# Issuing the first two loads of an add-and-GELU kernel ahead of the program's opening barrier

## The chip, the cores and the metric

The kernel runs on one core of a Trainium2 chip. The metric is the device time of one execution in microseconds (us); lower is better. The profile's span runs from the first to the last instruction that it shows. The device time is longer than the span (123.23 against 121.5 us before the change).

## The reference

```python
def reference(x, y):                       # both (1024, 4096) float32
    z = x + y
    return 0.5 * z * (1 + np.tanh(np.sqrt(2 / np.pi) * (z + 0.044715 * z ** 3)))
```

Two inputs of 16.8 MB are read and one output of 16.8 MB is written.

## The kernel before

Each of the 128 partitions holds 32768 numbers. The data are loaded in five pieces per input and stored in five pieces, all issued by SyncE on one queue (a transfer is issued when SyncE orders it, and lands when its last data have arrived). The compute goes through 32 chunks of 128x1024: an add on GpSimd (only the first chunk is on VectorE), a square on ScalarE, `scalar_tensor_tensor` on VectorE, a sigmoid on ScalarE, a multiply on VectorE. `z` has room for the whole problem; `y` has two buffers, so only the loads of the last two pieces of y (and their followers in the queue) wait for compute.

```python
    loads = [2048, 6144, 8192, 8192, 8192]      # columns per piece: 1, 3, 4, 4, 4 MB
    stores = [8192, 8192, 8192, 4096, 4096]
    ...
    pool_y = ctx.enter_context(tc.tile_pool(name="y", bufs=2))
    ...
    def load_x(i):
        a, b = lr[i]
        nc.sync.dma_start(out=zt[:, a:b], in_=xv[:, a:b])
    def load_y(i):
        ...
        nc.sync.dma_start(out=yt[s][:, o : o + b - a], in_=yv[:, a:b])
    ...
    sp = []
    for i in range(len(loads)):
        sp += [(load_x, i), (load_y, i)]
    sp += [(store, i) for i in range(len(stores))]
    ...
    with tc.manual_schedule():
        one = pool_sb.tile([P, 1], fp32, tag="one", name="one")
        nc.vector.memset(one, 0.0)
        nc.scalar.activation(out=one, in_=one, func=act.Sigmoid)   # brings the table load forward
        ...
```

What the source does not show is the opening that the framework puts before this. The programs here start with a head block: GpSimd fills four constants; each engine runs a `DRAIN` instruction ("drains" below) and takes part in a barrier (SyncE, ScalarE, VectorE and TensorE report to GpSimd, GpSimd releases them). Only then do the engines branch to the kernel's own instructions.

Of the kernel before, what the change touches and what calls it, by code (L numbers as in the profile page):

```python
# [1 line left out]

# [1 line left out]

# [4 lines left out]


@with_exitstack
def kernel(
    ctx: ExitStack,
    tc: tile.TileContext,
    x: bass.AP,
    y: bass.AP,
    out: bass.AP,
):








    nc = tc.nc
    P = nc.NUM_PARTITIONS
    fp32 = mybir.dt.float32
    act = mybir.ActivationFunctionType  # L30
    alu = mybir.AluOpType

    N, D = x.shape
    assert N % P == 0
    TOT = N // P * D
    xv, yv, ov = (a.rearrange("(p n) d -> p (n d)", p=P) for a in (x, y, out))

    c1 = 2.0 * math.sqrt(2.0 / math.pi)
    root = math.sqrt(c1 * 0.044715)

    YS = 8192
    CH = 1024
    PS = 4
    loads = [2048, 6144, 8192, 8192, 8192]
    stores = [8192, 8192, 8192, 4096, 4096]

    def ranges(sizes):
        ends = [sum(sizes[: i + 1]) for i in range(len(sizes))]
        assert ends[-1] == TOT
        return [(e - f, e) for e, f in zip(ends, sizes)]  # L50

    lr, sr, cr = ranges(loads), ranges(stores), ranges([CH] * (TOT // CH))
    C = len(cr)
    by_pool = set(range(1, C))

    def over(rs, lo, hi):
        return [i for i, (a, b) in enumerate(rs) if a < hi and b > lo]

    pool_sb = ctx.enter_context(tc.tile_pool(name="xz", bufs=1))
    pool_y = ctx.enter_context(tc.tile_pool(name="y", bufs=2))  # L60
    pool_w = ctx.enter_context(
        tc.tile_pool(name="w", bufs=PS, space=bass.MemoryType.PSUM)
    )

    zt = pool_sb.tile([P, TOT], fp32, tag="z", name="z")
    yt, wt = {}, {}
# [7 lines that stand above are left out]
        s, o = divmod(a, YS)  # L74
        if o == 0:
            yt[s] = pool_y.tile([P, YS], fp32, tag="y", name=f"y{s}")
        nc.sync.dma_start(out=yt[s][:, o : o + b - a], in_=yv[:, a:b])  # L77

    def store(i):
        a, b = sr[i]  # L80
        nc.sync.dma_start(out=ov[:, a:b], in_=zt[:, a:b])

    def add(c):
        a, b = cr[c]
        s, o = divmod(a, YS)
        eng = nc.gpsimd if c in by_pool else nc.vector
        eng.tensor_add(out=zt[:, a:b], in0=zt[:, a:b], in1=yt[s][:, o : o + b - a])  # L87

    def sq(c):
        a, b = cr[c]  # L90
        wt[c] = pool_w.tile([P, CH], fp32, tag="w", name=f"w{c}")
        nc.scalar.activation(  # L92
            out=wt[c], in_=zt[:, a:b], func=act.Square, scale=root
        )

    def stt(c):
        a, b = cr[c]
        nc.vector.scalar_tensor_tensor(  # L98
            out=wt[c], in0=wt[c], scalar=c1, in1=zt[:, a:b], op0=alu.add, op1=alu.mult
        )  # L100

    def sig(c):
        nc.scalar.activation(out=wt[c], in_=wt[c], func=act.Sigmoid)  # L103

    def mul(c):
        a, b = cr[c]
        nc.vector.tensor_mul(out=zt[:, a:b], in0=wt[c], in1=zt[:, a:b])  # L107
# [6 lines that stand above are left out]
    pool = [(add, c) for c in range(C) if c in by_pool]  # L114
    dve, acts = [], []
    for i in range(-3, C + 1):
        if 0 <= i < C:
            dve.append((stt, i))
            acts.append((sig, i))
        if 0 <= i - 1 < C:  # L120
            dve.append((mul, i - 1))
        if 0 <= i + 3 < C and i + 3 not in by_pool:
            dve.append((add, i + 3))
        if 0 <= i + 2 < C:
            acts.append((sq, i + 2))

    needs = {
        load_x: lambda i: [],
        load_y: lambda i: [
            (add, c)  # L130
            for c in over(cr, lr[i][0] - 2 * YS, lr[i][0] - YS)
            if lr[i][0] % YS == 0
        ],
        add: lambda c: [(f, i) for i in over(lr, *cr[c]) for f in (load_x, load_y)],
        sq: lambda c: [(add, c)] + ([(mul, c - PS)] if c >= PS else []),
        stt: lambda c: [(sq, c)],
        sig: lambda c: [(stt, c)],
        mul: lambda c: [(sig, c)],
        store: lambda i: [(mul, c) for c in over(cr, *sr[i])],
    }  # L140
    queues = [sp, pool, acts, dve]
    done = set()
# [3 lines that stand above are left out]
        nc.scalar.activation(out=one, in_=one, func=act.Sigmoid)  # L146
        while any(queues):
            moved = False
            for q in queues:
                while q and all(n in done for n in needs[q[0][0]](q[0][1])):  # L150
                    fn, arg = q.pop(0)
                    fn(arg)
                    done.add((fn, arg))
                    moved = True
                    if q is not sp:
                        break
            assert moved, [q[:1] for q in queues]


# [1 line left out]
_INS = ['x', 'y']  # L161
_OUTS = [((1024, 4096), 'float32')]


# [23 lines left out]
```

## Time and profile before

The time before was 123.27 us (median of 3 runs, 123.16 to 123.56).

| What | Value | Where it is read |
|---|---|---|
| DMA, share of 16 engines' span | 97.2% | queue table |
| VectorE / GpSimd / ScalarE busy | 62% / 60% / 52% | engine table |
| First load issued | 0.74 us | timeline |
| First add | 8.20 us | timeline |
| Span | 121.5 us | page |

From the page of the kernel before: the engines' busy time, the transfers in 40 equal slices of the span (tenths busy, then GB/s), the load and store queue (packets, MB, share), and the chain of work that ended last.

```profile
DVE 75.5 (62%) x66; ACT 63.8 (52%) x66; POOL 73.0 (60%) x35
...
DMA  3999999998989999999999999899999999999993
GB/s 89 421 440 494 413 389 494 391 496 367 496 378 486 389 475 389 475 389 475 389 475 389 475 389 475 345 432 434 424 432 432 442 421 442 421 442 389 426 437 130
...
q1 hardware_dynamic: 2160, 50.33, 97.2%
...
DMA 49%; POOL 17%; DVE 16%; SPq 2%; ACT 1%; issue 0%; POOLq 0%
```

Only the first and the last slice stand out in the DMA row. Between them the transfers never pause. The chain names GpSimd and VectorE for 33% of the span, but a chain follows one path back from the last instruction; it does not say that the queue beside it was idle, and the DMA row says that it wasn't.

The opening in the timeline of the kernel before (start, duration, engine, line, operation; in brackets the idle time before it and what ended it; SPq is SyncE's queue).

```profile
0.24 0.10 POOL L172 MEMSET const-float32-0.0<- 128x1 f32 x1 [0.24 <-issue]
...
0.73 1.28 ACT L146 ACT_TABLE_LOAD   x1 [0.73 <-PEq L172]
0.74 0.38 SPq L70 DMA_DIRECT2D z<-in_x_dram  x1
...
1.17 0.43 SPq L77 DMA_DIRECT2D y<-in_y_dram  x1
1.65 0.42 SPq L70 DMA_DIRECT2D z<-in_x_dram  x1
...
8.20 1.22 DVE L87 TENSOR_TENSOR z<-z,y 128x1024 f32<-128x1024 f32 x1 [7.33 <-DMA y<-in_y_dram]
```

The barrier's own instructions, in the view by source line of the kernel before (duration in ns as min/median/max, then first and last start in us).

```profile
L172 POOLq EVENT_SEMAPHORE  x2: 17/17/17, 0.5 to 0.6; - x2
L172 SPq DRAIN  x1: 7/7/7, 0.0 to 0.0; - x1
...
L172 POOLq DRAIN  x1: 186/186/186, 0.3 to 0.3; - x1
...
L172 SPq EVENT_SEMAPHORE  x1: 17/17/17, 0.7 to 0.7; - x1
```

SyncE drains at 0.0 us and has nothing to do until it is released at 0.7 us: GpSimd is still filling constants and draining. The loads need none of this.

### The profile page before, as it was taken

To read this page: it belongs to the slowest core of one execution; us is meant where nothing else is said; L and a number is where in the kernel's file an instruction comes from. 1 tells how busy PE (TensorE), PEld (TensorE's weight loads), DVE (VectorE), ACT (ScalarE), POOL (GpSimd) and SP (SyncE) were. 2 spreads that over 40 slices of the span, in tenths; PEclk is the share of its full clock that TensorE was granted. 3 is DMA by queue.
4 is the path that set the end of the run, shared out by engine and by line. 5 is a ranking of instruction groups with operands and counts; after the bars stand their busy time and mean duration, and the time that the engine had idled before them with its cause. 6 is when DMAs were issued, how large, how long until landed. Compare 5 with 4: busy or idle time off the path is not lost.

```text
span 121.5 us, 248 instructions
## 1 busy us (share of the span) xinstructions
DVE 75.5 (62%) x66; ACT 63.8 (52%) x66; POOL 73.0 (60%) x35
## 2 busy tenths in 40 slices
DVE  0035700039999209999996999995999999500000
ACT  4004400068886028788767887883878878100000
POOL 0028000499990099999969999959999990000000
DMA  3999999998989999999999999899999999999993
GB/s 89 421 440 494 413 389 494 391 496 367 496 378 486 389 475 389 475 389 475 389 475 389 475 389 475 345 432 434 424 432 432 442 421 442 421 442 389 426 437 130
DMA packets 2162, 50.35 MB, mean 415 GB/s; under 512 B 240, under 2 KB 240, under 8 KB 240
## 3 DMA queue, kind: packets, MB, share of 16 engines
q1 hardware_dynamic: 2160, 50.33, 97.2%
q14 instruction: 2, 0.02, 0.0%
HBM read 33.55 MB, written 16.78 MB: 414 GB/s over the span
## 4 chain that ended last, share of the span: by engine, by line
DMA 49%; POOL 17%; DVE 16%; SPq 2%; ACT 1%; issue 0%; POOLq 0%
DMA y<-in_y_dram 49%; POOL z L87 17%; DVE z L107 8%; DVE w L98 8%; SPq L70 1%; SPq L77 1%; ACT w L92 1%; POOLq L87 0%
## 5 line engine op out<-in xcount | busy, mean ns | idle before, releaser
L87 POOL TENSOR_TENSOR z<-z,y 128x1024 f32<-128x1024 f32 x31 | 72.8, 2389 | 26.9 <-DMA y<-in_y_dram 26.9
L92 ACT ACTIVATE w<-z 128x1024 f32<-128x1024 f32 x32 | 32.9, 1028 | 38.7 <-POOL z L87 31.4
L98 DVE SCALAR_TENSOR_TENSOR w<-w,z 128x1024 f32<-128x1024 f32 x32 | 39.4, 1232 | 21.1 <-ACT w L92 21.1
L107 DVE TENSOR_TENSOR z<-w,z 128x1024 f32<-128x1024 f32 x32 | 38.8, 1214 | 0.0
L103 ACT ACTIVATE w<-w 128x1024 f32<-128x1024 f32 x32 | 31.4, 981 | 0.4 <-DVE w L98 0.4
L87 DVE TENSOR_TENSOR z<-z,y 128x1024 f32<-128x1024 f32 x1 | 1.2, 1224 | 7.3 <-DMA y<-in_y_dram 7.3
L146 ACT ACT_TABLE_LOAD x1 | 1.3, 1283 | 0.7 <-PEq L172 0.7
L145 DVE MEMSET one<- 128x1 f32 x1 | 0.1, 59 | 0.8 <-PEq L172 0.8
L172 POOL MEMSET const-float32-0.0<- 128x1 f32 x1 | 0.1, 98 | 0.2 <-issue 0.2
L146 ACT ACTIVATE one<-one 128x1 f32<-128x1 f32 x1 | 0.2, 203 | 0.0
L172 POOL MEMSET const-bfloat16-1.0<- 128x1 bf16 x1 | 0.1, 101 | 0.0
L172 POOL MEMSET const-uint8-127<- 128x1 uint8 x1 | 0.1, 101 | 0.0
L172 POOL MEMSET const-float32-1.0<- 128x1 f32 x1 | 0.1, 98 | 0.0
## 6 DMA issues: line engine op xcount, KB each, us to landing
z<-in_x_dram SPq DMA_DIRECT2D x3, 4096.0 KB, 34.2
y<-in_y_dram SPq DMA_DIRECT2D x3, 4096.0 KB, 24.8
out_dram<-z SPq DMA_DIRECT2D x3, 4096.0 KB, 30.3
out_dram<-z SPq DMA_DIRECT2D x2, 2048.0 KB, 17.4
z<-in_x_dram SPq DMA_DIRECT2D x1, 3072.0 KB, 13.8
y<-in_y_dram SPq DMA_DIRECT2D x1, 3072.0 KB, 20.6
z<-in_x_dram SPq DMA_DIRECT2D x1, 1024.0 KB, 4.9
y<-in_y_dram SPq DMA_DIRECT2D x1, 1024.0 KB, 6.9
```

Of the source, the lines that this page charges most:

```text
L70: nc.sync.dma_start(out=zt[:, a:b], in_=xv[:, a:b])
L77: nc.sync.dma_start(out=yt[s][:, o : o + b - a], in_=yv[:, a:b])
L87: eng.tensor_add(out=zt[:, a:b], in0=zt[:, a:b], in1=yt[s][:, o : o + b - a])
L92: nc.scalar.activation(out=wt[c], in_=zt[:, a:b], func=act.Square, scale=root)
L98: nc.vector.scalar_tensor_tensor(out=wt[c], in0=wt[c], scalar=c1, in1=zt[:, a:b], op0=alu.add, op1=alu.mult)
L103: nc.scalar.activation(out=wt[c], in_=wt[c], func=act.Sigmoid)
L107: nc.vector.tensor_mul(out=zt[:, a:b], in0=wt[c], in1=zt[:, a:b])
L145: nc.vector.memset(one, 0.0)
L146: nc.scalar.activation(out=one, in_=one, func=act.Sigmoid)
L172: nc = _bacc.Bacc("TRN2", target_bir_lowering=False, num_devices=1)
```

## The change

The intent is to use those idle 0.7 us: the program is closed and compiled early, and then the first two load instructions are taken from SyncE's part of the body and put before SyncE's drain in the head block. They wait on no semaphore, which the code asserts.

```diff
+def begin_early(nc, count):
+    blocks = nc.main_func.blocks
+    head, body = blocks[0], blocks[1]
+    SP = mybir.EngineType.SP
+    queue = [i for i in body.instructions if i.engine == SP]
+    moved = [i for i in queue if isinstance(i, mybir.InstDMACopy)][:count]
+    assert not any(i.sync_info and i.sync_info.on_wait for i in moved)
+    at = next(k for k, i in enumerate(head.instructions) if i.engine == SP and isinstance(i, mybir.InstDrain))
+    for k, i in enumerate(moved):
+        body.instructions.remove(i)
+        head.instructions.insert(at + k, i)
 ...
             assert moved, [q[:1] for q in queues]
+    ctx.close()
+    tc.close()
+    tc.compile()
+    begin_early(nc, 2)
```

## The prediction

> **What bounds the kernel now.** The DMA engines. The queue table gives the load/store queue 97.2% of the 16 engines' span, 50.33 MB at 414 GB/s. The windows view shows their share at 0.92 to 1.10 in every 5 us stretch from 5 to 119 us. The Trainium skill (page "DMA: Bandwidth & Descriptors", section Specifications) puts the fabric ceiling of the 16 engines at 435 GB/s; the trace agrees (419 to 434 GB/s in most steady stretches). The compute engines have slack: VectorE 62%, GpSimd 60%, ScalarE 52%. The last store is issued at 104.8 us and lands 15.7 us later although its own 2 MB need about 5 us at that rate, so transfers stand in a queue to the end. The chain of waits says 49% DMA, then GpSimd and VectorE, but the queue beside it never empties, so I trust the windows.
>
> Outside full-rate transfer: the start (SyncE's first load is issued at 0.74 us, first bytes move at 1.6 us, full rate from about 3.0 us) and the end (bytes stop near 119.6 us, span 121.5 us).
>
> **Why the first issue is at 0.74 us.** View by source line, for the opening: SyncE's drain is at 0.0 us and takes 7 ns. SyncE then waits 0.7 us in the barrier (waits of its queue: 0.7 us, once), because GpSimd runs four memsets from 0.24 us and a drain of 0.19 us from 0.3 us, and only then gathers and releases (two semaphore events at 0.5 and 0.6 us).
>
> **What the change does.** It removes nothing. It moves two SyncE issues (1 MB of x, 0.38 us; 1 MB of y, 0.43 us) ahead of SyncE's drain, into those idle 0.7 us. They wait for nothing.
> - First issue: from 0.74 to about 0.03 us, a gain of 0.70 us. With the same 0.86 us from issue to bytes, data move from about 0.9 us.
> - Cost: SyncE drains at about 0.9 us, later than GpSimd's 0.5 us. The barrier opens at about 1.1 instead of 0.7 us. ScalarE's table load (1.28 us) and VectorE's memset start 0.4 us later; both have until the first adds, at 8.2 us before and about 7.5 us after. No cost.
> - Third load: issued at about 1.2 us instead of 1.65 us, well before the first 2 MB (5 us at full rate) are through. The queue doesn't run dry.
>
> **On the critical path:** all of the shift, since all that follows is paced by the DMA queue: 0.7 us, 0.6% of 123.27 us. The slow ramp from 1.6 to 3.0 us should move along; if part of it is tied to absolute time, up to 0.3 us are lost. Expected gain 0.65 us.
>
> Predicted: 122.6 us, 8 in 10 between 122.2 and 123.1 us. Chances: faster by over 2% 0.01, within 2% 0.97, slower by over 2% 0.02.
>
> **What would show each step.** Right: first load issued at 0.0 to 0.1 us, second near 0.45 us; first bytes near 0.9 us; barrier released near 1.1 us; third load near 1.2 us; first VectorE add near 7.5 us; last store issued near 104.1 us; span near 120.8 us. Wrong: first bytes still near 1.6 us; a pause in the transfers at 5 to 7 us (third load late); the early shift eaten by a lower rate later.
>
> **What would make it wrong.** SyncE's drain could wait until its two loads have landed (6.9 us for y before): then the third load comes at 6 to 7 us, the queue runs dry for 1 to 2 us, and the kernel is slower by about 1 us. The clock may start with SyncE's first instruction in a way that counts the early issue. Run-to-run spread (123.16 to 123.56 us) is over half of the gain.

## The result, and the profile after

The changed kernel took 122.56 us (median of 6 runs, 122.44 to 122.94) against 123.19 us for the kernel before (6 runs, 123.03 to 123.56). All outputs are right. The ratio is 0.9952, 95% interval 0.9933 to 0.9971, so the gain is real and small: within 2%. A ratio is the mean time of one kernel's runs over that of the other's of the same rounds, so it isn't quite the ratio of the medians quoted.

The same lines of the page of the kernel after:

```profile
DVE 75.5 (62%) x66; ACT 63.8 (53%) x66; POOL 73.0 (60%) x35
...
DMA  6999999999999989898989898998999999989992
...
q1 hardware_dynamic: 2160, 50.33, 97.8%
...
DMA 49%; POOL 17%; DVE 16%; SPq 1%; ACT 1%; issue 0%; POOLq 0%
```

The only clear change is in the first slice of the DMA row, from 3 tenths to 6. The opening in the timeline of the kernel after (line numbers are 15 higher in the kernel's body, as code was added above it):

```profile
0.00 0.38 SPq L85 DMA_DIRECT2D z<-in_x_dram  x1
0.23 0.10 POOL L192 MEMSET const-float32-0.0<- 128x1 f32 x1 [0.23 <-issue]
...
0.43 0.42 SPq L92 DMA_DIRECT2D y<-in_y_dram  x1
1.26 1.28 ACT L161 ACT_TABLE_LOAD   x1 [1.26 <-PEq L192]
1.26 0.33 SPq L85 DMA_DIRECT2D z<-in_x_dram  x1
...
7.48 1.22 DVE L102 TENSOR_TENSOR z<-z,y 128x1024 f32<-128x1024 f32 x1 [6.08 <-DMA y<-in_y_dram]
```

The first load is issued 0.74 us earlier and the first add comes 0.72 us earlier. The barrier opens later, near 1.2 instead of 0.7 us, because SyncE now reports to it last. The barrier's instructions in the view by source line of the kernel after show that, and one thing more:

```profile
L192 POOLq EVENT_SEMAPHORE  x2: 17/17/17, 1.1 to 1.1; - x2
...
L192 SPq DRAIN  x1: 125/125/125, 0.9 to 0.9; - x1
L192 SPq EVENT_SEMAPHORE  x1: 17/17/17, 1.2 to 1.2; - x1
```

SyncE's drain after the two issues takes 125 ns where it took 7 (131 ns after one moved load and 125 ns after seven, in the experiments below). It does not wait for the data: the first load landed only at 4.90 us.

Does the head start last to the end? The trace records, for each transfer, when each of its 16 parts landed; below is the time of the last part, in us from the span's start, taken from those records (not a view of the profile).

```
transfer             before     after   earlier by
first packet starts    1.74      1.01      0.72
x piece 1 (1 MB)       5.62      4.90      0.72
y piece 1 (1 MB)       8.10      7.38      0.72
y piece 2 (3 MB)      22.71     22.00      0.71
x piece 4 (4 MB)      51.86     51.14      0.72
x piece 5 (4 MB)      71.31     70.58      0.73
y piece 5 (4 MB)      81.53     81.06      0.47
store 1 (4 MB)        91.58     91.28      0.30
last store (2 MB)    120.56    120.26      0.30
```

Between 8 and 70 us the shift is constant in this pair: the transfers run like a conveyor belt, 4 MB every 9.72 us, which is 432 GB/s. In the stretch where the last load and the first stores share the engines, these two profiles lose 0.4 us of the shift. In part this is the choice of the pair: the profiled run of the change (122.94 us, span 121.2) was the slowest of its six, and the other five had spans of 120.7 to 121.0 us. Over all runs the mean gain is 0.6 us (0.0048 of 123.2). A shift as steady as this one between 8 and 70 us is in part this pair's luck. In the profiles of the experiments below with none and with two loads moved, the shift is 0.72 us at y piece 1, 0.37 at x piece 5 and 0.54 at the last store; and the profile with none moved is up to 0.3 us ahead of the one of the kernel before until x piece 5, though both issue alike. Two profiles show where the shift arises; its size comes from the times of all runs.

### The profile page after: what moved, and what is told of

Its sections match the earlier page's. It is cut to its first block, busy times and chain, and to the rows that moved or that the text cites. A ratio compares the mean times of both kernels' runs of the same rounds, so it can differ in the third digit from the quotient of the medians.

```text
span 121.2 us, 248 instructions
## 1 busy us (share of the span) xinstructions
DVE 75.5 (62%) x66; ACT 63.8 (53%) x66; POOL 73.0 (60%) x35
## 4 chain that ended last, share of the span: by engine, by line
DMA 49%; POOL 17%; DVE 16%; SPq 1%; ACT 1%; issue 0%; POOLq 0%
DMA y<-in_y_dram 49%; POOL z L102 17%; DVE z L122 8%; DVE w L113 8%; ACT w L107 1%; SPq L85 1%; SPq L92 1%; POOLq L102 0%
```

## The experiments

The theory: the time is the start of the first load plus a stretch of transfers without a gap, so the gain is the 0.7 us by which the first load is earlier; the later barrier is free because compute and the later issues have slack. Rivals: the gain comes from closing and compiling the program early; each moved load saves its own issue time; a late barrier costs what it is late; compute is on the critical path, as the chain suggests. All ratios are to the kernel before, run on the same chip in the same rounds.

### How many loads are moved

Four kernels that differ in one number:

```diff
-    begin_early(nc, 2)
+    begin_early(nc, 0)      # or 1, or 7; and 2 again
```

Nothing moved:

> The changed program with nothing moved (early closing and compiling kept). Theory (the gain is the earlier start of a transfer-bound queue): nothing moves, ratio to before 1.000 within 0.002, first load issued near 0.74 us. Rival (the gain comes from closing and compiling the program early, not from the loads): ratio near 0.995 as for the full change.

One load:

> Only the first load (1 MB of x) goes ahead of the barrier. Theory: what counts is when the first bytes flow, as long as the queue is fed from then on; 1 MB lasts 2.5 us and the second load is issued near 0.8 us, so the whole gain is there: ratio 0.994 to 0.996, equal to two moved within 0.001. Barrier released near 0.75 us. Rival (each load moved saves its own issue time, about 0.4 us): half of the gain, ratio near 0.9975.

All seven loads that wait for nothing:

> All seven loads that wait for nothing go ahead of the barrier, which then opens near 3.7 us. Theory: no further gain and no loss; ratio 0.994 to 0.996, equal to two moved; ScalarE's table load starts near 3.7 us and ends near 5.0 us, before the first add at 7.5 us. Rival 1 (each load moved saves issue time): ratio below 0.990. Rival 2 (a late barrier costs what it is late): slower than two moved by about 2.5 us, ratio near 1.015.

Two loads, the change itself, again:

> The change itself, on the same chip and in the same rounds as the other three. Theory: ratio 0.994 to 0.996, span shorter than the one of before by 0.6 to 0.8 us, first bytes near 0.9 to 1.0 us.

| Loads moved | Median us (5 runs) | Ratio, 95% interval | First load / barrier opens, us |
|---|---|---|---|
| before | 123.57 (9 runs) | 1 | 0.74 / 0.7 |
| 0 | 123.52 | 0.9997 (0.9985 to 1.001) | 0.73 / 0.7 |
| 1 | 122.84 | 0.9943 (0.9930 to 0.9955) | 0.00 / 0.7 |
| 2 | 122.72 | 0.9930 (0.9917 to 0.9942) | 0.00 / 1.2 |
| 7 | 122.90 | 0.9941 (0.9928 to 0.9955) | 0.00 / 3.7 |

The early compiling alone does nothing. Moving the first load alone brings the gain, and further loads add nothing that is clear of noise: the intervals of one, two and seven overlap. So what counts is the start of the first transfer, not the issue time of each. That a barrier at 3.7 us costs nothing (seven moved) is the first evidence for the slack. Three stated figures were missed, all narrowly: the change itself was expected at 0.994 to 0.996 and came out at 0.9930, its spans are shorter by 0.9 us by the medians (expected 0.6 to 0.8), and one load differs from two by 0.0013 in the ratio (expected within 0.001).

### A barrier made late on purpose

To see whether the start of the loads really sets the time one for one, and how much slack the rest has, GpSimd is made to fill a scratch tile several times ahead of its own drain. Each fill takes 1.0 us and all of them hold up the barrier.

```diff
+def late_pool(nc, count):            # moves the fills to before GpSimd's drain in the head block,
+    ...                              # in the way of begin_early
...
+        pad = pool_sb.tile([P, 1024], fp32, tag="pad", name="pad")
+        for _ in range(4):           # or 2, or 10
+            nc.gpsimd.memset(pad, 0.0)
...
+    late_pool(nc, 4)
-    begin_early(nc, 2)
+    begin_early(nc, 0)               # or 2, 3, 7
```

Four fills, nothing moved:

> Nothing moved, and GpSimd fills a scratch tile of 128x1024 four times ahead of its own drain, so that the barrier opens later by L (to be read from the trace; an estimate from the add's 2.39 us for the same tile is 2 to 8 us in all). Theory (the time is the start of the first load plus the transfers): the kernel is slower by L, within 0.3 us. Rival (the start of the compute or of the queue has slack, so that an early or late start of the loads is absorbed later): slower by clearly less than L.

Measured: 127.28 us against 123.27 us, ratio 1.0326 (1.0304 to 1.0347), so 4.01 us slower by the medians. The timeline of this kernel:

```profile
0.37 3.98 POOL L174 MEMSET pad<- 128x1024 f32 x4
4.65 1.28 ACT L176 ACT_TABLE_LOAD   x1 [4.65 <-PEq L208]
4.66 0.37 SPq L97 DMA_DIRECT2D z<-in_x_dram  x1
```

The first load is issued at 4.66 instead of 0.74 us, 3.92 us later, and the kernel is slower by the same amount within the noise. The late start of the queue is not absorbed anywhere.

Ten fills, seven loads moved:

> All seven loads without a wait moved, and ten fills, so the barrier opens about 2.5 times as late as with four. Theory: the queue is full for 50 us whatever the barrier does, and the compute catches up before the next load needs it; the time is that of the change, ratio 0.993 to 0.998. Rival (compute is on the critical path, as the chain of waits with its 33% of GpSimd and VectorE says): slower by the lateness of the first add against 7.2 us.

Measured: 122.80 us, ratio 0.9963 (0.9939 to 0.9987). Its timeline, from the issue of the last of the seven loads:

```profile
3.04 0.44 SPq L97 DMA_DIRECT2D z<-in_x_dram  x1
10.71 1.28 ACT L176 ACT_TABLE_LOAD   x1 [10.71 <-PEq L208]
...
10.86 1.23 DVE L114 TENSOR_TENSOR z<-z,y 128x1024 f32<-128x1024 f32 x1
...
22.05 2.34 POOL L114 TENSOR_TENSOR z<-z,y 128x1024 f32<-128x1024 f32 x1 [7.76 <-DMA y<-in_y_dram]
```

Here the barrier opens ten us late and the first add starts at 10.86 instead of 7.48 us, and the kernel is still as fast as the change within the noise (a loss of up to about 0.4 us is inside the interval). At 22.05 us GpSimd is already waiting for data again (for 7.76 us), so the delay has been swallowed. Together with the run before it this settles the question of the critical path for the opening: 3.9 us of delay cost 4.0 us when they delay the queue too, and a barrier ten us late, which delays only the compute engines (3.4 us at the first add, as its data land only at 7.3 us), costs nothing that can be measured.

Ten fills, two loads moved:

> Two loads moved and ten fills. Theory: the queue runs dry when 2 MB are through, near 6 us, until the third load's bytes come, about 0.9 us after its issue; the loss against the change is third issue plus 0.9 us less 6 us, within 0.5 us, and the seven-load kernel with the same late barrier is faster by that much. Rival (two loads ahead are enough whatever the barrier does, or compute alone sets the loss): no difference between the two.

Measured: 128.94 us, ratio 1.0454 (1.0433 to 1.0476), 6.1 us slower than with seven loads moved under the same late barrier. The stretches of its opening (start and end of the stretch, its length, the engines' busy time, clock, DMA share, GB/s):

```profile
5.00:6.00 1.00, 0.00 (x0) 0.00 (x0) 0.94 (x2) 1.00 1.06 451
6.00:7.00 1.00, 0.00 (x0) 0.00 (x0) 0.94 (x2) 1.00 0.55 229
7.00:8.00 1.00, 0.00 (x0) 0.00 (x0) 0.94 (x2) 1.00 0.00 0
8.00:10.00 2.00, 0.00 (x0) 0.00 (x0) 1.89 (x3) 1.00 0.00 0
10.00:11.00 1.00, 0.20 (x2) 0.29 (x1) 0.54 (x2) 1.00 0.00 0
11.00:12.00 1.00, 1.00 (x1) 0.99 (x1) 1.00 (x1) 1.00 1.46 369
```

The 2 MB are through at about 6.6 us, and the queue is dry until the third load, issued at 10.71 us, brings bytes. The formula of the expectation gives 10.71 + 0.9 - 6 = 5.6 us. The third transfer landed 5.57 us later than in the seven-load kernel (20.19 against 14.62 us in the landing records), as expected, but in part by luck. The packet records put the pause at only about 5.1 us (the parts of the 2 MB end at 6.72 us on average, the next begin at 11.79 us); the rest fits the first 16 packets after the pause, which took 1.54 us on average, against 0.91 us for such a packet in steady running. The formula had the end of the 2 MB too early and left out the slow packets. Another 0.4 us was added later, where loads and stores overlap, and the total missed the stated 0.5 us narrowly.

Four fills, two loads moved:

> Two loads moved, and the same four fills, so the barrier opens L later than GpSimd alone would open it. Theory: as long as the third load is issued before the first two (2 MB) are through at about 6 us, the late barrier costs nothing and the time is that of the change, ratio to before 0.993 to 0.997; if the barrier opens after that, the loss is third issue plus 0.9 us less about 6 us. Rival (the late barrier costs what it is late, by way of ScalarE, VectorE and the later loads): slower than the change by about L.

Measured: 123.53 us, ratio 1.0028 (1.0004 to 1.0053). This missed the expectation. The third load was issued at 4.66 us, two us before the first 2 MB were through, and yet the kernel is 0.7 us slower than the seven-load kernel of the same rounds; all four runs (123.44 to 124.00 us) are above all four of that one (122.59 to 123.03). Its third issue in the timeline, and the stretches of its opening, which show no pause:

```profile
4.66 0.33 SPq L97 DMA_DIRECT2D z<-in_x_dram  x1
...
5.00:6.00 1.00, 0.00 (x0) 0.99 (x2) 0.00 (x0) 1.00 1.06 451
6.00:7.00 1.00, 0.00 (x0) 0.15 (x1) 0.00 (x0) 1.00 1.47 582
7.00:8.00 1.00, 0.66 (x1) 0.00 (x0) 0.62 (x1) 1.00 0.86 369
```

(The view counts a packet whole in the stretch in which it starts, so a stretch of 1 us can show a share above 1.00.) The mean over the 16 DMA engines hides what went wrong. The 16 landings of the third transfer, from the trace's records, in us:

```
seven moved, ten fills   14.16 ... 14.40 14.42 14.50 14.51 14.62
two moved, four fills    14.21 ... 14.42 14.43 14.44 14.46 15.15
```

Fifteen parts are on time; one is 0.70 us behind the next, and it stays behind by 0.70 to 0.72 us in every transfer down to the ninth, then by more: it lands the last store at 120.78 us when the others are done by 119.82. A transfer is complete only when all its parts have landed, so one late engine carries its lateness to the end. (The records do not name the engine; that it is one and the same within this run is read from the one part that is late by the same amount each time.) A packet of 24 KB takes 0.912 us in steady running; at the hand-over one that started at 6.89 us took 1.22 us and one that started at 8.10 us, so right behind it, took 1.26 us, together 0.66 us more.

Two more runs ask whether the nearly empty queue or the late barrier was to blame. Two fills, two loads moved:

> Two loads moved and two fills of 1 us, so the barrier opens near 2.6 us and the third load is issued near 2.7 us, 4 us before the first 2 MB are through. With four fills (third load at 4.66 us) the kernel lost 0.7 us against seven loads moved. Theory (the third load came too close to the end of the queue and one DMA engine started it late): no loss here, ratio 0.993 to 0.997. Rival (a late barrier itself costs in proportion): half of the loss, ratio near 0.999 to 1.000.

Four fills, three loads moved:

> Three loads moved (5 MB, which last until about 14 us) and the same four fills as before, so the barrier opens at 4.6 us again and the fourth load is issued then. Theory (it is the nearly empty queue): no loss, ratio 0.993 to 0.997, and the 16 landings of each load end within 0.5 us of each other. Rival (the late barrier, by whatever way): the loss of the kernel with two moved and four fills stays, ratio near 1.002.

Measured: two fills, 122.94 us, ratio 0.9953 (0.9933 to 0.9973), with the third load issued at 2.64 us; four fills and three loads, 122.75 us, ratio 0.9940 (0.9920 to 0.9961), with the barrier again at 4.65 us. From the timelines, the third load with two fills, then the third and fourth loads with four fills and three loads moved:

```profile
2.64 0.33 SPq L97 DMA_DIRECT2D z<-in_x_dram  x1
...
0.89 0.43 SPq L97 DMA_DIRECT2D z<-in_x_dram  x1
4.66 0.33 SPq L104 DMA_DIRECT2D y<-in_y_dram  x1
```

In the latter kernel the 16 landings of every load are within 0.5 us (0.39 us for the third). The barrier was as late as in the kernel that lost 0.7 us, and the loss is gone, so the lateness of the barrier itself was not it; it was the third load being issued too close to the end of what was queued. Why one of the 16 engines took the hand-over badly is not settled, and only one profile of that kernel exists; that the loss is in all four of its runs is measured, that it is the same engine each time is not.

### Attempts at a better version

Large pieces first:

```diff
-    loads = [2048, 6144, 8192, 8192, 8192]
+    loads = [6144, 2048, 8192, 8192, 8192]
```

> The change with the first two pairs of loads swapped in size, so 3 MB of x and 3 MB of y go first (rows of 24 KB instead of 8 KB) and the first add starts near 15 us. Theory (the queue sets the time, compute has slack): between equal to the change and 0.3 us faster, as the slow first packets carry more bytes; ratio 0.991 to 0.996. Rival (an early first add matters): slower than the change by over 1 us.

Measured: 122.59 us, ratio 0.9927 (0.9907 to 0.9946). The first add starts at 16.94 us (near 15 was expected) instead of 7.48 us and nothing is lost, which is a second, independent sign that compute has slack. The interval overlaps those of the change, so it can't be called faster than the change.

The first two loads on two queues at once:

```diff
-        nc.sync.dma_start(out=yt[s][:, o : o + b - a], in_=yv[:, a:b])
+        q = nc.scalar if i == 0 else nc.sync
+        q.dma_start(out=yt[s][:, o : o + b - a], in_=yv[:, a:b])
...
-    begin_early(nc, 2)
+    begin_early(nc, mybir.EngineType.SP, 1)            # takes the engine as an argument here
+    begin_early(nc, mybir.EngineType.Activation, 1)
```

> The first load of x is moved ahead on SyncE, the first of y on ScalarE's queue, also ahead of the barrier, so that both are issued at 0.0 to 0.1 us. Theory (the first bytes set the time; they come about 1.0 us after the issue and the first packets of each engine are slow whatever is queued behind): equal to the change within 0.2 us, ratio 0.992 to 0.997. Rival (the issue time of the second load is part of the start-up): faster than the change by up to 0.4 us, ratio near 0.991.

Measured: 122.78 us, ratio 0.9943 (0.9924 to 0.9961), although the load of y was issued at 0.12 us: no gain over one queue. The Trainium skill (page "DMA: Bandwidth & Descriptors", section "Issuing engines are not separate DMA queues") says that starting transfers from several engines saves only the time of their issue; this run agrees. Even the issue time saved brought nothing that can be measured; the change, too, has issued both loads (by 0.85 us) before the first packets of the first one start (1.01 us). But the run is no clean test of an earlier second load. By the packet records the first packet of ScalarE's queue started only at 2.65 us, and with the next load of SyncE's queue beside it the first y landed at 9.78 instead of 7.38 us; the first add came at 9.88 us, and that cost nothing either. Why ScalarE's queue began so late is not settled.

## Why the prediction was right

- **The total.** 122.6 us was predicted with a gain of 0.65 us; 122.56 us was measured, and over the runs of the change the gain was 0.6 us in the first set (ratio 0.9952) and 0.9 us in the second (0.9930 of 123.57). So the size is right, but that the total was met to 0.04 us is luck.
- **What bounds the kernel.** The prediction trusted the unbroken transfers over the chain of waits. The delayed kernels confirm it: delay before the queue starts costs one for one (3.92 us late, 4.01 us slower), delay of compute alone at the opening costs nothing that can be measured (3.4 us late at the first add, ratio 0.9963).
- **The start.** The first load was issued at 0.00 and the second at 0.43 us, as predicted. First bytes "near 0.9 us" were at 1.01 us: the 0.86 us from issue to bytes had been read from stretches of 0.2 us. The packet records give 1.00 us before (0.74 to 1.74) and 1.01 us after. The latency was underestimated by 0.14 us, but it moved along, and the difference of 0.7 us is what counts.
- **The barrier.** It was put at 1.1 us and the third load at 1.2 us; measured are 1.18 (SyncE's release) and 1.26 us. The term that was too small is SyncE's drain, taken as 7 ns and measured at 125 ns after the issues. It was free, as predicted.
- **The feared cases.** SyncE's drain did not wait for the data, and the queue did not run dry. The margin for the latter is smaller than the prediction thought: it asked only that the third load come before 2 MB are through at 6 us, and a third load at 4.66 us already cost 0.7 us. The clock did not count the early issue differently: in both profiled runs the device time is 1.8 us longer than the span.
- **The end.** The last store was predicted to be issued near 104.1 us and the span to be near 120.8 us; the profile has 104.4 and 121.2 us, while the other five runs have spans of 120.7 to 121.0 us. The 0.4 us by which this profile falls short arise between 70 and 92 us, where the last load meets the first stores. That this stretch varies from run to run is seen; why is not settled.

## What to carry to other kernels

If the queue of transfers runs without a gap from start to end, as here, the kernel's time is the moment of its first issue plus a constant, so a load that waits for nothing should be the very first instruction of its engine, ahead of any start-up barrier; moving one load is enough if the next follows while much is still queued. Before counting on such a gain, check that the transfers are really unbroken: a deliberate delay, once before the queue and once before the compute only, shows in two runs which of them sets the time. Keep several us of work queued ahead at every hand-over (here 4 us were enough and 2 us were not), and look at the landings of each of the 16 parts, as one late engine was invisible in the mean here and lasted to the end.

## What the Trainium skill lacked or had wrong

- "DMA: Bandwidth & Descriptors", sections Specifications and "Latency and other measured facts": they give about 0.6 us to the first byte for transfers issued by SyncE. Here the first packet started 1.00 us after the issue began (0.74 to 1.74 us before the change, 0.00 to 1.01 us after), of which 0.38 us are the issue itself. The figure agrees if it is counted from the end of the issue (0.62 us); the page doesn't say from where it counts.
- Same page, Specifications: the HBM limit of about 358 GB/s per core did not bind; the loads ran at 432 GB/s (4 MB in 9.72 us), near the 435 GB/s of the fabric. "Perfetto Trace Analysis", section Roofline, has this case right: one core alone can exceed its share. (This program ran on one core; the record does not say whether the other core of its pair was idle.)
- No page says that the first packets of an idle queue are slow: the first 16 packets took 0.80 us on average before the change and 0.95 us after, against 0.309 us (the median) for the same 8 KB in steady running. After the pause of 5 us above, the first 16 packets of 24 KB took 1.54 us, against 0.912 us.
- No page says how much must still be queued when the next transfer is issued: a load issued about 2 us before the queue's end cost 0.7 us, one issued 4 us before cost nothing. "DMA: Bandwidth & Descriptors", section "Why a DMA increments its semaphore by 16 and not by 1", explains why one late engine suffices for this, and the trace agrees (15 parts by 14.46 us, the last at 15.15 us).
- "Runtime: NRT & Kernel Launch", section "The ~15µs preamble/postamble breakdown", tells of the runtime's barriers but not of the barrier that the program itself opens with, which held the first load back to 0.74 us; nor does any page say what a drain takes right after transfers have been issued on the same engine (125 to 131 ns here, against 7 without).
